# Row halves in turn in the first mixer's score and transpose groups, and the inverse's transfers issued by GpSimd

## The chip, the cores and the metric

The kernel runs on one core of a Trainium2 chip. The metric is the time of one execution on the device in microseconds (us), of which the median over several runs is given. Times inside the program come from one profiled execution of the kernel before; its clock starts with the first instruction of the span.

## The reference, cut to what matters

The program is a two-layer decoder trunk on an input of 1024 tokens by 1024 features, all in float32. Layer 0 is a mixer of eight retention heads and eight RWKV-7 heads, layer 1 is windowed attention, and each is followed by a feed-forward block.

```
for layer in (0, 1):
    h = rms_norm(x)
    x = x + (mixer(h) if layer == 0 else attention(h))
    x = x + swiglu(rms_norm(x))
return rms_norm(x)

mixer(h):
    z = h @ w_in                     # 4*512 columns for retention, 3*512+256 for RWKV
    ret = group_norm(chunk_retention(rotary(q), rotary(k), v)) * silu(g)
    y = rwkv7_scan(r, decay, k, v, -kk, kk * a)
    rwkv = (group_norm(y) + bonus) * gate
    return concat(ret, rwkv) @ w_out

rwkv7_scan, for each token t and head:
    sa = S @ a_t
    S  = S * w_t + outer(sa, b_t) + outer(v_t, k_t)
    y_t = S @ r_t
```

The change touches only how the RWKV-7 heads of `mixer` are computed. The scan is done there in chunks of 64 tokens. In a chunk, the four products of the rows (`AR`: decayed a and r) with the columns (`BK`: decayed b and k) are one matrix product, a "score"; the recursion within the chunk is then the inverse of a unit triangular 64x64 matrix.

## The kernel before, in words

**Stages.** The mixer takes the first 640 us of the 2289 us span, then come the feed-forward block, attention and the second feed-forward block. The sequence is cut in two halves of 512 tokens, and the eight RWKV heads into four pairs of two heads: a head of a pair lies on partitions 0 to 63 (row half e=0), the other on 64 to 127 (e=1). Two pairs of one half of the sequence make a `unit`, so there are units 0 to 3; each inverts the triangles of its two pairs and then runs the recursion.

**Order of TensorE.** All matmuls of the mixer are emitted by generators that the planner `Plan.run` lets advance, but the order in which TensorE executes them is written out in a table, `PE_ORDER`. `pe_order` walks it and ties each matmul behind the one before. A token names a stream, the number of an output tile in that stream, and a count: `i5,6:4` takes the next four matmuls of tiles 5 and 6 of stream i alternately, `i5:2` two of tile 5 alone. Stream F is the mixer's projections (24 matmuls of 128x512 each). Streams f to m are the eight `pair` generators (f, g for unit 0; h, i for unit 1; j, k for unit 2; l, m for unit 3), b to e the four units, n to u the retention pairs. Ahead of the table `pe_order` also ties five single matmuls behind others ("pins"); these lines are the same in both kernels.

**Tiles of a pair.** In a `pair` stream, tiles 5 and 6 are the scores of chunks 0 to 3 for row half e=0 and e=1 (4 matmuls `ps_m<-AR,BK` of 64 rows by 128 each), tiles 7 and 8 the same for chunks 4 to 7, and tiles 9 and 10 the transposes of `BK`, 8 for each row half (`ps_m<-c_ident,BK`, issued by the helper `tr`, L304; the helper `mm`, L293, issues the other matmuls).

**A unit's inverse.** `unit` loads the triangles in 32x32 blocks into `DT`, runs 31 substitution steps on VectorE, writes the blocks `X` to DRAM (`dg`, L976, two transfers), clears the two tiles `GT` on GpSimd (L981), and reads the blocks back into their places with eight transfers (L985). Each has 8x32 pieces of 128 B, 32 KB in all. VectorE transposes `TZ<-GT` (L995, four of them), TensorE multiplies `ps_c<-TZ,GG` (tiles 0 and, from the copies of it, 1 of the unit stream, 32 matmuls for each pair), ScalarE copies, and so on. Each engine takes its instructions strictly in order; the transfers of one issuing queue as well.

**Names.** `qd` is the retention query times its decay (GpSimd, L1199, in place in `r`); TensorE uses it in `ps_m<-r,Sc`. `rr`, `rkk`, `rv` with `z` and `zlast` are the token shift of the RWKV inputs (L756 to L760). `hc<-n` (L1451) are four transfers of attention-layer data that GpSimd issues after the mixer.

Of the kernel before, what the change touches and what calls it, by code (L numbers as in the profile page):

```python
# [10 lines left out]
F32 = mybir.dt.float32  # L11
# [92 lines left out]

PE_ORDER = """
F0:13 F1:2 F0:3 F1:14 F0:3 F1:3 F0:3 F1:3 F0:2 F1:2 F2:2 a0:1 F2:22 F3:24 f0:1 f1:1 F4:24 F5:24 F6:15 f2:1 F6:9
F7:24 g0:1 g1:1 F8:9 f3:16 F8:9 g2:1 F8:6 F9:18 f4:1 F9:6 F10:6 f5,6:8 f7,8:8 F10:17 f9:8 f10:8 f11:16 f12:4
g3:16 f13:4 n0:4 n1:4 g4:1 F10:1 F11:12 f14:16 g5:1 g6:2 g5:2 g6,5:3 g7:1 g8:2 g7:2 F11:12 F12:3 g8,7:3 g9:8
g10:8 F12:13 g11:16 g12:4 n2,3:8 g13:4 F12:8 F13:5 n4:8 n5:8 F13:16 n6:8 g14:16 F13:3 F14:21 n7:1 F14:3 F15:24
F16:6 o0:4 o1:4 F16:18 F17:3 o2,3:8 o4:8 F17:21 o5:1 o6:1 o5:7 b0:32 o6:7 h0:1 h1:1 F18:18 b1:32 o7:1 F18:6  # L110
F19:12 b2:8 h2:1 b3:8 b4:8 F19:12 b5:8 b6:16 b7:8 b8:8 F20:24 F21:13 b9:16 b10:8 h3:16 b11:8 b12:4 F21:8 i0:1
i1:1 b13:4 F21:3 F22:24 F23:6 b14:4 i2:1 F23:6 b20:1 b15:4 b20:15 b21:6 b16:4 b21:4 b22:16 b23:5 F23:9 b23:1
b21:2 b17:4 b23:6 h4:1 F23:3 F24:11 b21:1 b18:4 b21:1 b23:2 h5:4 b21:1 b19:4 b21:1 b23:2 F24:12 h6:4 b24:1 F24:1
F25:24 F26:7 b25:1 b26:1 h7:4 h8:4 b27:1 h9:8 F26:11 h10:8 h11:16 h12:4 i3:16 h13:4 p0:4 F26:6 F27:9 p1:4 i4:1
p2:2 p3:2 p2,3:4 h14:16 i5,6:4 i5:2 i6:2 i7:4 i8:4 F27:15 F28:2 p4:8 i9:8 i10:8 F28:6 i11:16 i12:4 p5:8 p6:8
i13:4 F28:16 F29:19 v0:1 p7:1 i14:16 F29:5 F30:7 q0:4 q1:4 F30:3 F31:2 F30:3 F31:11 q2,3:8 F30:9 F31:6 F30:2
F31:2 q4:8 q5:8 F31:3 F32:6 q6:8 F32:18 F33:22 q7:1 c0:32 F33:2 F34:23 c1:32 F34:1 F35:20 c2:8 c3:8 c4:8 j0:1
F35:4 F36:11 j1:1 c5:8 c6:16 c7:8 c8:8 j2:1 F36:9 c9:16 c10:8 c11:8 c12:2 F36:4 F37:10 c12:2 F37:14 F38:7 j3:5
c13:4 j3:11 k0:1 k1:1 F38:8 c20:5 c14:4 c20:11 c21:6 c22:1 c21:2 c15:4 c22:15 c23:4 c21:2 c23:1 c16:4 c23:5 k2:1
F38:9 F39:8 c17:4 c21:2 c23:2 j4:1 F39:16 F40:2 c21:1 c18:4 c21:1 c23:2 j5:4 c21:1 c19:4 c21:1 c23:2 F40:3 j6:4  # L120
F40:19 F41:12 c24:1 F41:12 F42:24 c25:1 c26:1 j7,8:8 c27:1 j9:8 F43:13 j10:8 j11:16 j12:4 k3:16 j13:4 k4:1
F43:11 F44:11 j14:16 k5,6:8 k7:4 k8:4 F44:9 k9:8 k10:8 k11:16 k12:4 r0:4 r1:4 F44:4 F45:10 k13:4 r2,3:8 r4:8
F45:12 k14:16 r5:8 r6:8 l0:1 l1:1 F45:2 F46:17 r7:1 l2:1 F46:7 F47:24 m0:1 m1:1 F48:24 F49:1 l3:1 F49:17 d0:1
l3:3 d0:31 l3:12 m2:1 d1:32 F49:6 F50:15 d2:8 d3,4:16 d5:8 F50:9 F51:2 d6:16 d7:8 m3:16 d8:8 d9:16 d10:8 d11:8
F51:8 s0,1:8 d12:4 F51:14 F52:2 d13:4 F52:19 s2:1 d14:4 s3,2:7 F52:3 F53:3 d15:4 s4:8 F53:18 s5:2 d16:4 s6:8
d20:3 s5:6 d17:4 d20:13 d21:13 d18:4 d21:1 d22:16 d23:3 d21:1 d19:4 d21:1 d23:13 l4:1 F53:3 F54:14 m4:1 s7:1
l5:3 l6:3 l5:1 l6:1 d24:1 F54:10 F55:17 d25:1 d26:1 F55:7 F56:9 l7:4 l8:4 d27:1 l9:8 l10:8 l11:16 l12:4 m5:3
m6:3 m5:1 m6:1 l13:4 F56:15 m7:2 m8:2 m7,8:4 m9:8 m10:8 t0:4 t1:4 F57:24 m11:16 m12:4 t2:4 e0:2 t3:4 l14:16
m13:4 t4:8 t5:8 t6:4 e0:4 m14:1 t6:4 m14:15 e0:26 F58:24 F59:15 t7:1 e1:32 u0:4 u1:4 F59:9 W0:7 e2:8 e3:8 e4:8
u2:4 W0:17 W1:11 u3:4 e5:8 u4:8 e6:16 e7:8 e8:8 u5:8 u6:8 e9:16 e10:8 e11:8 e12:2 u7:1 e20:5 e12:2 e20:11 e21:4  # L130
e22:6 e13:4 e22:10 e23:4 e21:2 e14:4 e23:2 W1:13 W2:14 e15:4 e21:1 W2:10 W3:13 e21:1 e23:2 e21:1 e16:4 e21:1
e23:2 W3:11 W4:9 e17:4 e21:2 e23:2 W4:15 W5:4 e21:1 e18:4 e21:1 e23:2 W5:20 e19:4 e21:2 W6:24 W7:3 e23:2 e24:1
e25:1 e26:1 e27:1 W7:21
"""


# [121 lines left out]
class Kern:  # L258
# [686 lines left out]
    def unit(self, u, hf, pairs):  # L945

        nc, mp = self.nc, self.mp
        V, S, G = nc.vector, nc.scalar, nc.gpsimd
# [33 lines left out]
        for q in range(8):  # L982
            e, b = (q // 2) % 2, q % 2
            r0 = 64 * e + 32 * b
            nc.sync.dma_start(  # L985
                GTs[q // 4][r0 : r0 + 32, :, 32 * b : 32 * b + 32], dg[q * 8 : q * 8 + 8].rearrange("c s t -> s c t")
            )
        yield tuple((f"a{u}_{p}", 0.0) for p in pairs), 6.0
# [1061 lines left out]
```

## Time and profile before

| | before |
|---|---|
| median of 3 runs | 2292.93 us (2291.54 to 2293.13) |
| profiled execution, device time | 2291.26 us |
| its span, first to last instruction | 2289.4 us |
| granted TensorE clock | 0.999 |
| TensorE busy | 2259.3 us (99% of the span) |
| VectorE, ScalarE, GpSimd busy | 1699.6, 1047.6, 1009.2 us |
| TensorE busy in 0 to 640 us | 624.41 us |
| GpSimd busy in 0 to 640 us | 157.06 us |

A row of a timeline gives the start in us, the length of a run of like instructions, engine, source line, operation, output and inputs, the shape and a count. In square brackets stands how long the engine was idle before it and what released it. A row of a tile view gives the durations of one instruction as minimum/median/maximum in ns, and the first and last start. Line numbers are those of the kernel before; the changed kernel's are one lower from there on, since its table has one line less.

### The profile page before, as it was taken

Reading aid. Unit: us, or ns where it says so; the run is one execution under the profiler, and the core shown is the slowest. Engines: PE = TensorE matmul, PEld = TensorE weight load, DVE = VectorE, ACT = ScalarE, POOL = GpSimd, SP = SyncE. Lnnn points to the kernel's source line nnn. Section 1 sums busy time; section 2 is a strip of 40 time slices with the busy share of each in tenths; the row PEclk is TensorE's granted clock in tenths of the full one; section 3 lists DMA queues with packets and bytes.
Section 4 is the critical chain, followed back from the end, with each engine's and each line's share of the span. In section 5 each row is a group of like instructions: output and inputs, shape, how many; then the busy total and the mean of one; then the engine's idle time right before and its main releaser. Section 6 shows DMA issues by size and latency. Waiting matters only on the chain.

```text
span 2289.4 us, 35743 instructions
## 1 busy us (share of the span) xinstructions
PE 2259.3 (99%) x13056; PEld 1808.5 (79%) x13056; DVE 1699.6 (74%) x2635; ACT 1047.6 (46%) x1947; POOL 1009.2 (44%) x796
## 2 busy tenths in 40 slices
PE   8999999999999999999999999999999999999998
PEld 6777777778878888888788887787788888888886
DVE  7877965876567268887895958857657788888866
ACT  5454544434445333334343466657744333333335
POOL 3123221212340167777776501113203677777675
PEclk9999999999999999999999999999999999999999
DMA  7566554444356455565756332133246466657663
GB/s 279 187 214 210 193 163 128 145 119 132 134 185 221 170 177 205 203 212 211 280 212 239 110 120 79 44 99 118 93 140 230 169 217 213 210 196 284 230 216 116
DMA packets 170336, 406.43 MB, mean 178 GB/s; under 512 B 43184, under 2 KB 45872, under 8 KB 170160
## 3 DMA queue, kind: packets, MB, share of 16 engines
q1 hardware_dynamic: 166752, 397.59, 50.7%
q10 hardware_dynamic: 2832, 4.45, 0.5%
q8 instruction: 104, 1.70, 0.3%
q0 software_dynamic: 576, 2.10, 0.2%
q14 instruction: 72, 0.59, 0.1%
HBM read 275.48 MB, written 123.21 MB: 174 GB/s over the span
## 4 chain that ended last, share of the span: by engine, by line
PE 79%; DVE 10%; ACT 4%; issue 3%; DMA 2%; SPq 1%; POOL 1%; DVEq 0%; ACTq 0%; POOLq 0%
PE ps_f L293 10%; PE ps_m L1302 7%; PE ps_m L1304 7%; PE ps_m L1305 7%; PE ps_m L293 6%; PE ps_f L1302 5%; PE ps_f L1304 5%; PE ps_f L1305 5%; PE ps_f L452 2%; PE ps_f L449 2%; PE ps_f L451 2%; PE ps_r L1302 2%; PE ps_c L1305 2%; PE ps_r L1304 2%; PE ps_c L1304 2%
## 5 line engine op out<-in xcount | busy, mean ns | idle before, releaser
L293 PE MATMUL ps_f<-n,w 128*128 128x512 f32 x1440 | 359.2, 403 | 8.3 <-ACT w L434 5.7
L293 PEld LDWEIGHTS ps_f<-n,w 128*128 128x128 f32 x1440 | 267.4, 189 | 83.0 <-issue 12.6
L435 POOL TENSOR_TENSOR w<-wr,w 128x512 fp32r<-128x512 f32 x63 | 87.0, 1388 | 301.4 <-ACT w L434 293.7
L434 ACT CAST w<-wr 128x512 fp32r<-128x512 f32 x231 | 141.2, 617 | 162.2 <-PE ps_f L452 54.2
L435 DVE TENSOR_TENSOR w<-wr,w 128x512 fp32r<-128x512 f32 x168 | 118.8, 710 | 61.4 <-ACT w L434 60.8
L1302 PE MATMUL ps_f<-n,w 128*128 128x512 f32 x415 | 164.3, 396 | 0.0
L1304 PE MATMUL ps_f<-n,w 128*128 128x512 f32 x415 | 162.7, 392 | 0.0
L1305 PE MATMUL ps_f<-n,w 128*128 128x512 f32 x415 | 162.5, 392 | 0.0
L435 POOL TENSOR_TENSOR w<-wq,w 128x512 fp32r<-128x512 f32 x91 | 130.8, 1448 | 30.9 <-ACT w L434 30.9
L1302 PE MATMUL ps_m<-n,w 128*128 128x512 f32 x333 | 130.4, 392 | 0.0
L1304 PE MATMUL ps_m<-n,w 128*128 128x512 f32 x333 | 129.7, 389 | 0.0
L1305 PE MATMUL ps_m<-n,w 128*128 128x512 f32 x333 | 129.5, 389 | 0.0
L1312 DVE TENSOR_TENSOR nq<-ps_m,u 128x512 f32<-128x512 f32 x88 | 58.9, 684 | 93.8 <-PE ps_m L1305 93.8
L1732 POOL TENSOR_SCALAR s<-s,st 128x256 f32<-128x256 f32 (+1 forms) x32 | 30.7, 961 | 191.1 <-ACT w L434 60.9
L466 POOL TENSOR_TENSOR n<-nq,n 128x512 fp32r<-128x512 f32 x60 | 100.0, 1679 | 7.6 <-ACT n L464 7.6
L1497 POOL TENSOR_TENSOR w<-wd,w 128x512 fp32r<-128x512 f32 (+1 forms) x62 | 87.7, 1423 | 33.5 <-ACT w L1496 31.5
L1302 PEld LDWEIGHTS ps_f<-n,w 128*128 128x128 f32 x415 | 77.9, 188 | 20.4 <-issue 3.8
L1302 PE MATMUL ps_m<-cb,w 128*128 128x512 f32 x236 | 91.9, 389 | 0.4 <-DVE nq L1312 0.4
L1304 PEld LDWEIGHTS ps_f<-n,w 128*128 128x128 f32 x415 | 77.9, 188 | 17.7 <-issue 2.0
L1305 PE MATMUL ps_m<-cb,w 128*128 128x512 f32 x236 | 91.8, 389 | 0.0
L1304 PE MATMUL ps_m<-cb,w 128*128 128x512 f32 x236 | 91.8, 389 | 0.0
L1305 PEld LDWEIGHTS ps_f<-n,w 128*128 128x128 f32 x415 | 77.9, 188 | 16.8 <-issue 0.7
(521 smaller groups left out, 6498.6 us busy)
## 6 DMA issues: line engine op xcount, KB each, us to landing
hc<-n SPq DMA_DIRECT2D x84, 512.0 KB, 3.2
wsp<-w SPq DMA_DIRECT2D x54, 512.0 KB, 3.3
w<-wsp SPq DMA_DIRECT2D x54, 512.0 KB, 3.4
n<-hc SPq DMA_DIRECT2D x54, 512.0 KB, 6.2
wq<-in_w_gate SPq DMA_DIRECT2D x44, 512.0 KB, 4.6
u<-u SPq DMA_DIRECT2D x88, 256.0 KB, 3.3
ha<-hc SPq DMA_DIRECT2D x34, 512.0 KB, 5.3
hid<-n SPq DMA_DIRECT2D x66, 256.0 KB, 2.1
```

The source lines that it names most:

```text
L293: i = self.nc.tensor.matmul(out, lhsT, rhs, **kw)
L434: nc.scalar.copy(hi[:, :n], raw[:, c])
L435: self.lo.tensor_tensor(out=lo[:, :n], in0=raw[:, c], in1=hi.bitcast(F32)[:, :n], op=ALU.subtract)
L449: x = nc.tensor.matmul(ps, hi, rh, start=k == 0, stop=False)
L451: y = nc.tensor.matmul(ps, hi, rl, start=False, stop=False)
L452: z = nc.tensor.matmul(ps, lo, rh, start=False, stop=k == n - 1)
L466: e.tensor_tensor(out=lo, in0=src, in1=hi.bitcast(F32), op=ALU.subtract)
L1302: i = mm(ps, hi, xh, start=first and k == 0, stop=False, skip_group_check=True)
L1304: mm(ps, hi, xl, start=False, stop=False, skip_group_check=True)
L1305: mm(ps, lo, xh, start=False, stop=last and k == len(w) - 1, skip_group_check=True)
L1312: self.last_add = V.tensor_tensor(out=o, in0=x, in1=y, op=ALU.add)
L1497: nc.gpsimd.tensor_tensor(out=lo, in0=v, in1=hi.bitcast(F32), op=ALU.subtract)
```

## The change

Two things change. In `PE_ORDER`, the score groups (tiles 5 and 6, 7 and 8) and the transposes (9 and 10) of the pair streams take the two row halves in turn, at most of the places where they ran one half after the other or in a mixed order. Untouched are f5 to f8, tiles 5, 6, 9 and 10 of h, all of j, and k5,6. In `unit`, the eight transfers `GT<-dg` are issued by GpSimd (`G` is `nc.gpsimd`) in place of SyncE. The table is re-wrapped, so the diff is shown by its tokens:

```
 pair  before                              after
 f     f9:8 f10:8                          f9,10:16
 g     g5:1 g6:2 g5:2 g6,5:3               g5,6:8
       g7:1 g8:2 g7:2 ... g8,7:3           g7,8:5 ... g7:1 g8:2
       g9:8 g10:8                          g9,10:16
 h     h7:4 h8:4                           h7,8:8
 i     i5,6:4 i5:2 i6:2 i7:4 i8:4          i5,6:8 i7,8:8
       i9:8 i10:8                          i9,10:16
 k     k7:4 k8:4 ... k9:8 k10:8            k7,8:8 ... k9,10:16
 l     l5:3 l6:3 l5:1 l6:1                 l5,6:8
       l7:4 l8:4 ... l9:8 l10:8            l7,8:8 ... l9,10:16
 m     m5:3 m6:3 m5:1 m6:1                 m5,6:8
       m7:2 m8:2 m7,8:4 m9:8 m10:8         m7,8:8 m9,10:16
```

```
@@ unit @@
         for q in range(8):
             e, b = (q // 2) % 2, q % 2
             r0 = 64 * e + 32 * b
-            nc.sync.dma_start(
+            G.dma_start(
                 GTs[q // 4][r0 : r0 + 32, :, 32 * b : 32 * b + 32], dg[q * 8 : q * 8 + 8].rearrange("c s t -> s c t")
             )
```

How the instructions stand on TensorE at pair l's second score group and its transposes, before; `ps_m_5490` and `5491` are tiles 7 and 8, `5518` and `5528` tiles 9 and 10:

```order
1577 L293 MATMUL ps_f_5706<-n_456_2935,w_5551 128x512
1578 L293 MATMUL ps_m_5490<-AR_4573,BK_4577 128x128 x4
1579 L293 MATMUL ps_m_5491<-AR_4573,BK_4577 128x128 x4
1580 L293 MATMUL ps_m_5508<-gl_3160,gup_163 128x512
1581 L304 MATMUL ps_m_5518<-c_ident_154,BK_4577 128x64 x8
1582 L304 MATMUL ps_m_5528<-c_ident_154,BK_4577 128x64 x8
```

The same place on TensorE in the changed kernel:

```order
1660 L292 MATMUL ps_f_5706<-n_456_2935,w_5551 128x512
1661 L292 MATMUL ps_m_5490<-AR_4573,BK_4577 128x128
1662 L292 MATMUL ps_m_5491<-AR_4573,BK_4577 128x128
1663 L292 MATMUL ps_m_5490<-AR_4573,BK_4577 128x128
1664 L292 MATMUL ps_m_5491<-AR_4573,BK_4577 128x128
1665 L292 MATMUL ps_m_5490<-AR_4573,BK_4577 128x128
1666 L292 MATMUL ps_m_5491<-AR_4573,BK_4577 128x128
1667 L292 MATMUL ps_m_5490<-AR_4573,BK_4577 128x128
1668 L292 MATMUL ps_m_5491<-AR_4573,BK_4577 128x128
1669 L292 MATMUL ps_m_5508<-gl_3160,gup_163 128x512
1670 L303 MATMUL ps_m_5518<-c_ident_154,BK_4577 128x64
1671 L303 MATMUL ps_m_5528<-c_ident_154,BK_4577 128x64
```

The same eight score matmuls and the same sixteen transposes stand between the same neighbours; only the tile, and with it the row half, now changes with each instruction.

On GpSimd, at unit 0's inverse, before (`X_2530` is the next unit's block tile, which is cleared here, `r_221_1310` the retention query that is multiplied by its decay):

```order
50 L1239 TENSOR_TENSOR r_211_1216<-r_211_1216,r_177_963 128x512
51 L1129 TENSOR_TENSOR r_220_1308<-r_220_1308,c_cos_242 128x512
52 L960 MEMSET X_2530 128x512
53 L962 MEMSET X_2530 64x16 x2
54 L758 COPY zlast_99<-z_1447 128x1
55 L759 TENSOR_TENSOR rr_1446<-z_1447 128x512
56 L1199 TENSOR_TENSOR r_221_1310<-r_221_1310,c_qdec_1393 128x512
```

The same place on GpSimd in the changed kernel (`dg_213` is what the inverse wrote to DRAM):

```order
50 L1238 TENSOR_TENSOR r_211_1216<-r_211_1216,r_177_963 128x512
51 L1128 TENSOR_TENSOR r_220_1308<-r_220_1308,c_cos_242 128x512
52 L984 DMA GT_1422<-dg_213 32x8x32 x4
53 L984 DMA GT_1423<-dg_213 32x8x32 x4
54 L959 MEMSET X_2530 128x512
55 L757 COPY zlast_99<-z_1447 128x1
56 L758 TENSOR_TENSOR rr_1446<-z_1447 128x512
57 L1198 TENSOR_TENSOR r_221_1310<-r_221_1310,c_qdec_1393 128x512
```

Unit 0's eight transfers now stand ahead of the clearing of `X`, of `rr` and of the query's product. In the other units they stand likewise among GpSimd's instructions: in unit 1 ahead of the clearing of `X` and of `rr`, in unit 2 behind `rkk` and ahead of the copy into `z`, the clearing of `X`, `PC` and `AR`, in unit 3 four and four around the product L1239. On SyncE the eight rows `GT<-dg` of each unit are gone; what stood behind them moves up.

More of the change, by code (lines that the diff above doesn't have):

```diff
@@ L106 @@
 F0:13 F1:2 F0:3 F1:14 F0:3 F1:3 F0:3 F1:3 F0:2 F1:2 F2:2 a0:1 F2:22 F3:24 f0:1 f1:1 F4:24 F5:24 F6:15 f2:1 F6:9
[L107 to L130, printed above, removed]
@@ L131 @@
-e22:6 e13:4 e22:10 e23:4 e21:2 e14:4 e23:2 W1:13 W2:14 e15:4 e21:1 W2:10 W3:13 e21:1 e23:2 e21:1 e16:4 e21:1
-e23:2 W3:11 W4:9 e17:4 e21:2 e23:2 W4:15 W5:4 e21:1 e18:4 e21:1 e23:2 W5:20 e19:4 e21:2 W6:24 W7:3 e23:2 e24:1
-e25:1 e26:1 e27:1 W7:21
+F7:24 g0:1 g1:1 F8:9 f3:16 F8:9 g2:1 F8:6 F9:18 f4:1 F9:6 F10:6 f5,6:8 f7,8:8 F10:17 f9,10:16 f11:16 f12:4 g3:16
+f13:4 n0:4 n1:4 g4:1 F10:1 F11:12 f14:16 g5,6:8 g7,8:5 F11:12 F12:3 g7:1 g8:2 g9,10:16 F12:13 g11:16 g12:4
+n2,3:8 g13:4 F12:8 F13:5 n4:8 n5:8 F13:16 n6:8 g14:16 F13:3 F14:21 n7:1 F14:3 F15:24 F16:6 o0:4 o1:4 F16:18
@@ new lines @@
+F17:3 o2,3:8 o4:8 F17:21 o5:1 o6:1 o5:7 b0:32 o6:7 h0:1 h1:1 F18:18 b1:32 o7:1 F18:6 F19:12 b2:8 h2:1 b3:8 b4:8
+F19:12 b5:8 b6:16 b7:8 b8:8 F20:24 F21:13 b9:16 b10:8 h3:16 b11:8 b12:4 F21:8 i0:1 i1:1 b13:4 F21:3 F22:24 F23:6
+b14:4 i2:1 F23:6 b20:1 b15:4 b20:15 b21:6 b16:4 b21:4 b22:16 b23:5 F23:9 b23:1 b21:2 b17:4 b23:6 h4:1 F23:3
+F24:11 b21:1 b18:4 b21:1 b23:2 h5:4 b21:1 b19:4 b21:1 b23:2 F24:12 h6:4 b24:1 F24:1 F25:24 F26:7 b25:1 b26:1
+h7,8:8 b27:1 h9:8 F26:11 h10:8 h11:16 h12:4 i3:16 h13:4 p0:4 F26:6 F27:9 p1:4 i4:1 p2:2 p3:2 p2,3:4 h14:16
@@ new lines @@
+i5,6:8 i7,8:8 F27:15 F28:2 p4:8 i9,10:16 F28:6 i11:16 i12:4 p5:8 p6:8 i13:4 F28:16 F29:19 v0:1 p7:1 i14:16 F29:5
+F30:7 q0:4 q1:4 F30:3 F31:2 F30:3 F31:11 q2,3:8 F30:9 F31:6 F30:2 F31:2 q4:8 q5:8 F31:3 F32:6 q6:8 F32:18 F33:22
+q7:1 c0:32 F33:2 F34:23 c1:32 F34:1 F35:20 c2:8 c3:8 c4:8 j0:1 F35:4 F36:11 j1:1 c5:8 c6:16 c7:8 c8:8 j2:1 F36:9
+c9:16 c10:8 c11:8 c12:2 F36:4 F37:10 c12:2 F37:14 F38:7 j3:5 c13:4 j3:11 k0:1 k1:1 F38:8 c20:5 c14:4 c20:11
+c21:6 c22:1 c21:2 c15:4 c22:15 c23:4 c21:2 c23:1 c16:4 c23:5 k2:1 F38:9 F39:8 c17:4 c21:2 c23:2 j4:1 F39:16
@@ new lines @@
+F40:2 c21:1 c18:4 c21:1 c23:2 j5:4 c21:1 c19:4 c21:1 c23:2 F40:3 j6:4 F40:19 F41:12 c24:1 F41:12 F42:24 c25:1
+c26:1 j7,8:8 c27:1 j9:8 F43:13 j10:8 j11:16 j12:4 k3:16 j13:4 k4:1 F43:11 F44:11 j14:16 k5,6:8 k7,8:8 F44:9
+k9,10:16 k11:16 k12:4 r0:4 r1:4 F44:4 F45:10 k13:4 r2,3:8 r4:8 F45:12 k14:16 r5:8 r6:8 l0:1 l1:1 F45:2 F46:17
+r7:1 l2:1 F46:7 F47:24 m0:1 m1:1 F48:24 F49:1 l3:1 F49:17 d0:1 l3:3 d0:31 l3:12 m2:1 d1:32 F49:6 F50:15 d2:8
+d3,4:16 d5:8 F50:9 F51:2 d6:16 d7:8 m3:16 d8:8 d9:16 d10:8 d11:8 F51:8 s0,1:8 d12:4 F51:14 F52:2 d13:4 F52:19
@@ new lines @@
+s2:1 d14:4 s3,2:7 F52:3 F53:3 d15:4 s4:8 F53:18 s5:2 d16:4 s6:8 d20:3 s5:6 d17:4 d20:13 d21:13 d18:4 d21:1
+d22:16 d23:3 d21:1 d19:4 d21:1 d23:13 l4:1 F53:3 F54:14 m4:1 s7:1 l5,6:8 d24:1 F54:10 F55:17 d25:1 d26:1 F55:7
+F56:9 l7,8:8 d27:1 l9,10:16 l11:16 l12:4 m5,6:8 l13:4 F56:15 m7,8:8 m9,10:16 t0:4 t1:4 F57:24 m11:16 m12:4 t2:4
+e0:2 t3:4 l14:16 m13:4 t4:8 t5:8 t6:4 e0:4 m14:1 t6:4 m14:15 e0:26 F58:24 F59:15 t7:1 e1:32 u0:4 u1:4 F59:9 W0:7
+e2:8 e3:8 e4:8 u2:4 W0:17 W1:11 u3:4 e5:8 u4:8 e6:16 e7:8 e8:8 u5:8 u6:8 e9:16 e10:8 e11:8 e12:2 u7:1 e20:5
@@ L134 @@
+e12:2 e20:11 e21:4 e22:6 e13:4 e22:10 e23:4 e21:2 e14:4 e23:2 W1:13 W2:14 e15:4 e21:1 W2:10 W3:13 e21:1 e23:2
+e21:1 e16:4 e21:1 e23:2 W3:11 W4:9 e17:4 e21:2 e23:2 W4:15 W5:4 e21:1 e18:4 e21:1 e23:2 W5:20 e19:4 e21:2 W6:24
+W7:3 e23:2 e24:1 e25:1 e26:1 e27:1 W7:21
 """
@@ L984, in unit @@
             r0 = 64 * e + 32 * b
-            nc.sync.dma_start(
+            G.dma_start(
                 GTs[q // 4][r0 : r0 + 32, :, 32 * b : 32 * b + 32], dg[q * 8 : q * 8 + 8].rearrange("c s t -> s c t")
```

## The prediction

> **What bounds the kernel now.** I first read the page's busy line and then the windows that part the span at the end of the first mixer (each engine: busy us and instructions).
>
> ```profile
> PE 2259.3 (99%) x13056; PEld 1808.5 (79%) x13056; DVE 1699.6 (74%) x2635; ACT 1047.6 (46%) x1947; POOL 1009.2 (44%) x796
> 0.00:640.00 640.00, 624.41 (x5590) 487.43 (x5590) 458.32 (x951) 293.47 (x475) 157.06 (x190) 1.00 0.53 171
> 640.00:2290.00 1650.00, 1634.87 (x7468) 1321.04 (x7466) 1241.23 (x1685) 754.16 (x1472) 852.11 (x606) 1.00 0.52 180
> ```
>
> TensorE is the bound nearly everywhere. The mixer leaves it 15.6 us idle, GpSimd (POOL) works only 157 of 640 us there. Next I read what TensorE waits for, in the mixer and behind it.
>
> ```profile
> PE ps_f L293 <- ACT w L434: 5.7, 1, 5.7
> PE ps_m L293 <- DVE r L1193: 2.0, 4, 1.3
> PE ps_f L293 <- DVE n L581: 1.7, 2, 1.0
> PE ps_c L293 <- DVE GT L1070: 1.4, 1, 1.4
> PE ps_c L293 <- DVE TZ L995: 0.2, 1, 0.2
> PE ps_m L1742 <- POOL s L1732: 0.9, 3, 0.5
> ```
>
> The largest wait is the start (5.7 us). The transfers that the change moves hold TensorE up for 0.2 us in all, through `TZ`. Behind the mixer the longest entry is 0.9 us, so the later layers have no idle time to swallow a shift: what TensorE gains or loses by the end of the mixer stays to the end. The clock is full throughout (1.00). So the sum has two kinds of terms: matmul groups that get shorter, and waits that GpSimd, now with 32 transfers to issue, makes for TensorE.
>
> **Row halves in turn.** The windows below count only the score matmuls (`AR` an input), with TensorE's busy time and their number. In order they are f5–8, h7,8, i5–8, k5–8, l5,6, l7,8, m5,6 and m7,8.
>
> ```profile
> 73.70:75.80 2.10, 2.04 (x32) 1.00 0.63 208
> 225.30:227.00 1.70, 1.65 (x16) 1.00 0.94 258
> 242.70:245.45 2.75, 2.71 (x32) 1.00 1.03 274
> 401.50:404.10 2.60, 2.57 (x32) 1.00 0.81 244
> 509.70:511.20 1.50, 1.43 (x16) 1.00 0.75 161
> 523.70:525.45 1.75, 1.68 (x16) 1.00 0.59 190
> 529.50:531.00 1.50, 1.46 (x16) 1.00 0.27 102
> 534.95:536.00 1.05, 1.02 (x16) 1.00 0.10 35
> ```
>
> The counts are records, two for a matmul. Where halves alternate already, 16 records take 1.02 us and 32 take 2.04; one half after the other, 16 take 1.65 to 1.68. So alternation takes 0.63 to 0.66 us off a group that ran half by half: h7,8 0.63; i 2.71 − 2.04 = 0.67; k 0.53; l5,6 0.41 and l7,8 0.66; m5,6 0.44; m7,8, largely in turn before, nothing. g's groups were mixed by ones and twos; I give them 0.1.
>
> For the transposes no alternated group exists. The windows are of 8 of one half (h9) and of both halves in sequence (i9,10).
>
> ```profile
> 228.00:228.80 0.80, 0.71 (x8) 1.00 1.04 425
> 250.10:251.20 1.10, 1.02 (x16) 1.00 0.00 0
> ```
>
> If the halves overlap fully, sixteen take what eight take, 0.71; if not at all, 1.02. I take 0.31 us off each of f, g, i, k, l and m, since the score groups do overlap; zero is the other end, 1.9 us in all. The raw sum is 0.31 (f) + 0.41 (g) + 0.63 (h) + 0.98 (i) + 0.84 (k) + 1.38 (l) + 0.75 (m) = 5.3 us.
>
> **What a transfer costs GpSimd.** Before, SyncE issues them; the rows are `GT<-dg` (256 pieces of 128 B), SyncE's transfers of 128 pieces, and the only transfers GpSimd issues, `hc<-n`, 128 pieces of 4 KB, with their landing times.
>
> ```profile
> L985 SPq DMA_DIRECT2D GT<-dg x32: 303/448/1338, 137.9 to 521.2; - x32
> DMA to landing us min/median/max: 1.7/2.3/4.7
> L412 SPq DMA_DIRECT2D w<-wsp x54: 319/326/609, 287.2 to 543.5; - x54
> L1451 POOL DMA_DIRECT2D hc<-n x4: 573/598/739, 1086.2 to 2060.7; - x4
> DMA to landing us min/median/max: 2.9/3.0/3.1
> ```
>
> GpSimd is held 0.598 us by a transfer of 128 pieces. With t for one of ours: if the price goes by transfer, t = 0.60; if by piece, 2 × 0.598 = 1.19. SyncE's ratio of the two kinds is 448/326 = 1.37, so I take t = 0.598 × 1.37 = 0.82, an estimate nearer the low row since the same shapes give that ratio on the one engine where both are seen. Eight hold GpSimd 6.6 us.
>
> The Trainium skill ("DMA: Bandwidth & Descriptors", section "Anatomy of one DMA — SWDGE (gpsimd) path") says that descriptor generation is small and that many descriptors can be emitted before their cost shows. By that, t would be the low end, 0.60; no run here shows a transfer of small pieces issued by GpSimd.
>
> **Unit 0.** The timeline rows of GpSimd behind the inverse's write to DRAM, then two of TensorE:
>
> ```profile
> 137.23 0.53 POOL L960 MEMSET X<- 128x512 f32 x1 [4.62 <-DMA dg<-X]
> 137.81 0.29 POOL L962 MEMSET X<- 64x16 f32 x2
> ...
> 138.69 1.04 POOL L759 TENSOR_TENSOR rr<-z 128x512 f32<-128x512 f32 x1
> 139.69 1.29 POOL L1199 TENSOR_TENSOR r<-r,c_qdec 128x512 f32<-128x512 f32 x1
> ...
> 142.39 0.43 PE L293 MATMUL ps_m<-r,Sc 64*64 64x128 f32 x2
> 144.94 0.69 PE L293 MATMUL ps_c<-TZ,GG 32*32 32x32 f32 x30 [0.22 <-DVE TZ L995]
> ```
>
> `dg` lands at 137.2. Before, the decayed query is done at 139.69 + 1.29 = 140.98 and TensorE takes it at 142.39 without a wait. In the changed order the eight transfers stand ahead of `X`, `rr` and the query; one small clearing (0.29 + gap) now falls behind it, so it is done at about 140.5 + 8t, and TensorE waits 8t − 1.9 us: 2.9 at 0.60, 4.7 at 0.82, 7.6 at 1.19. `TZ` (last issue 137.2 + 7t, landing 2.3 to 3.0, 0.44 to transpose) is ready about when the query is, and hides behind it. VectorE, with `TZ` now ahead of `rr` L760, has its weights' conversions late by less than that. What f and g gain (0.72) lies before this wait, which runs from the inverse's chain on VectorE, and is counted at nothing.
>
> **Unit 1.** GpSimd's first row behind the write, the last transpose of `TZ`, and TensorE's use of it:
>
> ```profile
> 296.02 0.53 POOL L960 MEMSET X<- 128x512 f32 x1 [1.32 <-DMA dg<-X]
> 300.90 0.44 DVE L995 STREAM_TRANSPOSE TZ<-GT 32x256 f32<-32x256 f32 x1 [0.42 <-DMA GT<-dg]
> 301.33 1.20 PE L293 MATMUL ps_c<-TZ,GG 32*32 32x32 f32 x64
> ```
>
> TensorE needs the second half of `TZ` in mid-group, near 301.9. Now the last transfer is issued at 296.0 + 7t, lands some 2.5 later (between the two rows), and 0.44 goes to the transpose: 298.9 + 7t, so a wait of 7t − 3.0 (1.2, 2.7, 5.3). h's 0.63 comes ahead of the triangles and is kept; i's 0.98 comes behind them, brings TensorE to the wait sooner, and is lost in it.
>
> **Units 2 and 3.** SyncE's issue in unit 2, TensorE's use, and the last transpose and the first use in unit 3:
>
> ```profile
> 439.39 3.77 SPq L985 DMA_DIRECT2D GT<-dg  x8
> 449.35 0.82 PE L293 MATMUL ps_c<-TZ,GG 32*32 32x32 f32 x40
> 525.36 0.44 DVE L995 STREAM_TRANSPOSE TZ<-GT 32x256 f32<-32x256 f32 x1
> 546.17 0.25 PE L293 MATMUL ps_c<-TZ,GG 32*32 32x32 f32 x4
> ```
>
> In unit 2 the last landing moves to about 439.4 + 7t + 2.5 = 447.6, the transpose to some 448.6 behind the copy into `z` that now waits for GpSimd: in time at 0.82, about 1.3 us late at 1.19. k's 0.84 may be met by that or by short waits for VectorE; I keep half, 0.4. Unit 3 has 20 us to spare, and l's and m's 2.1 us stay. Queues: SyncE loses 32 issues of 0.45 us, so that the loads behind them (`w<-wsp` and unit 3's rotary copies `r<-r`) go earlier; I give 0.4 for the short waits on them, with zero as the other end. GpSimd's rows behind its transfers are those named: `X`, `rr`, the query in unit 0, `z`, `PC`, `AR` in unit 2.
>
> **Sum.** At t = 0.82: +4.7 + 2.7 − 0.6 − 0.4 − 2.1 − 0.4 = +3.9 us. On the profiled execution of 2291.26 us that is 2295.2; the median, 1.67 us above it, becomes 2296.8. At 0.60 the sum is 2.9 + 1.2 − 3.5 = +0.6; at 1.19 7.6 + 5.3 + 1.3 − 3.1 = +11.1 (k's gain lost too).
>
> **The rivals.** *Price by transfer alone*: t = 0.60, +0.6 us, 2293.5. For it: 0.598 is the only price of GpSimd's that the trace shows. Against: SyncE's own price rises with the pieces. It is the skill's rule that stands above.
>
> *Price by piece (slower)*: t = 1.19 at GpSimd in units 0 and 1 makes TensorE wait 7.6 and 5.3 us; +11.1, 2304.0. It decides for slower from t = 0.87 on, where the sum passes 4.6 us. For it: software that writes pieces one at a time would do this. Against: nothing that the trace holds; it has one shape only.
>
> *Price by bytes (faster)*: `hc<-n` moves 512 KB for 0.598, ours 32 KB. If most of that goes with bytes, t is near 0.25 (a guess of order, between nothing and 0.60): unit 0 waits 0.1, unit 1 not, i's gain is kept, and the sum is 0.1 − 0.6 − 1.0 − 0.8 − 2.1 − 0.4 = −4.8, 2288.1. Against: it needs the query within 1.9 us of what it has now.
>
> *The halves in turn don't save what they show*: without the 3.1 us that the sum counts for them, +7.0, 2299.9. Against: eight windows say otherwise.
>
> **Numbers.** Forecast (t between 0.70 and 0.95, +2.1 to +5.8, 2295.0 to 2298.7) 0.38; by transfer 0.18; by piece 0.30; by bytes 0.10; no saving 0.04. A change within 0.2%, 4.6 us, is about what a measurement of this kernel can't tell from none. The forecast case lies two thirds within it: same 0.25 + 0.18 = 0.43, slower 0.13 + 0.30 + 0.04 = 0.47, faster 0.10. The range leaves out the faster rival and the far end of the by-piece one: 2290.5 to 2304.
>
> **What would show it.** GpSimd's rows `GT<-dg`: their mean is t. TensorE's waits: a new one before `ps_m<-r,Sc` near 142 on GpSimd's query, and one on `TZ` near 302. Score windows of 16 records at 1.02 us, transposes of 16 at 0.71. I am wrong if the query's wait is under 2 us or above 7, if unit 2 makes TensorE wait by over 1 us, or if the groups keep their old length.

## The result, and the profile after

| | before | after |
|---|---|---|
| median | 2293.03 us (2291.54 to 2295.17, 4 runs) | 2314.93 us (2312.10 to 2315.82, 4 runs) |
| ratio, 95% interval | | 1.0096 (1.0084 to 1.0108) |
| profiled execution, span | 2291.26, 2289.4 us | 2312.10, 2310.3 us |
| granted TensorE clock | 0.999 | 0.993 |

The changed kernel is about 22 us slower, far outside the forecast range that ended at 2304. The waits of TensorE in the mixer of the changed kernel (engine, tile and line, what it waited for: us in all, times, longest) show three entries, of 8.2, 6.4 and 3.2 us, that were 0.2 us or less before:

```profile
PE ps_m L292 <- POOL r L1198: 8.2, 1, 8.2
PE ps_c L292 <- DVE TZ L994: 6.4, 5, 1.8
PE ps_m L303 <- DVE GG L886: 3.2, 3, 2.4
```

A ledger by place comes from one group that stands once in each unit, TensorE's second inverse product. Its start in units 0 to 3 before, and then after:

```profile
151.93 1.20 PE L293 MATMUL ps_c<-GT,TZ 32*32 32x32 f32 x64
308.36 1.20 PE L293 MATMUL ps_c<-GT,TZ 32*32 32x32 f32 x64
452.37 1.20 PE L293 MATMUL ps_c<-GT,TZ 32*32 32x32 f32 x64
563.58 1.20 PE L293 MATMUL ps_c<-GT,TZ 32*32 32x32 f32 x64
```
```profile
163.49 1.20 PE L292 MATMUL ps_c<-GT,TZ 32*32 32x32 f32 x64
324.25 1.20 PE L292 MATMUL ps_c<-GT,TZ 32*32 32x32 f32 x64
473.41 1.20 PE L292 MATMUL ps_c<-GT,TZ 32*32 32x32 f32 x64
586.22 1.20 PE L292 MATMUL ps_c<-GT,TZ 32*32 32x32 f32 x64
```

TensorE is 11.6 us late behind unit 0, 15.9 behind unit 1, 21.0 behind unit 2 and 22.6 behind unit 3. At the end of the program the span is 20.9 us longer: as forecast, the later layers take little back (1.7 us). Such a ledger compares two single executions, and they differ by themselves: two of the kernels below, the order alone and unit 3 alone, are the same up to unit 3, and yet stand 1.5 us apart behind unit 0 and 3.9 behind unit 2. So differences of 2 to 4 us between two traces prove nothing unless a wait shows them.

**Unit 0.** The timeline of GpSimd in the changed kernel, from the landing of `dg`, two rows of VectorE, and the transfers in the tile view (durations in ns):

```profile
138.23 1.98 POOL L984 DMA_DIRECT2D GT<-dg  x3 [5.47 <-DMA dg<-X]
143.52 1.16 POOL L984 DMA_DIRECT2D GT<-dg  x2 [3.31 <-issue]
146.10 1.79 POOL L984 DMA_DIRECT2D GT<-dg  x3 [1.42 <-issue]
147.88 0.54 POOL L959 MEMSET X<- 128x512 f32 x1
...
149.49 1.26 POOL L1198 TENSOR_TENSOR r<-r,c_qdec 128x512 f32<-128x512 f32 x1
```
```profile
143.23 0.43 DVE L994 STREAM_TRANSPOSE TZ<-GT 32x256 f32<-32x256 f32 x1 [2.38 <-DMA GT<-dg]
145.81 0.43 DVE L994 STREAM_TRANSPOSE TZ<-GT 32x256 f32<-32x256 f32 x1 [1.39 <-DMA GT<-dg]
```
```profile
L984 POOL DMA_DIRECT2D GT<-dg x32: 582/584/814, 138.2 to 546.7; - x32
```

One transfer holds GpSimd 0.584 us, near the 0.60 of the rival "by transfer" and under the forecast 0.82. But after three of them it stands for 3.31 us and again for 1.42. Its own row names no releaser ("issue"), but the rows of VectorE do: the first `TZ` needs the first transfer and starts with its landing at 143.23, and GpSimd issues the fourth at 143.52; the second `TZ` needs the third transfer, starts at 145.81, and the sixth is issued at 146.10. So three transfers are under way, and the next one goes out 0.3 us after one of them has landed; the other three units show the same. It is not VectorE's work that holds GpSimd up, for VectorE is idle for 2.38 of the 3.31 us. The eight take 9.65 us (138.23 to 147.88), 1.2 us each. TensorE, in the rows below, waits 8.19 us for the query, and then runs every group at about twice its length (the 14 took 1.09 us before):

```profile
150.80 0.69 PE L292 MATMUL ps_m<-r,Sc 64*64 64x128 f32 x2 [8.19 <-POOL r L1198]
151.41 1.97 PE L292 MATMUL ps_m<-r,r 128*64 128x128 f32 x14
153.31 1.92 PE L292 MATMUL ps_c<-TZ,GG 32*32 32x32 f32 x64
```
```profile
152.00:159.00 7.00, 7.00 (x94) 0.50 0.04 11
```

The window's row shows why (its stretch, length, TensorE's busy time and records, then the granted clock, 0.50). From windows of 1 us each, half clock begins at 145.70, in the middle of the wait, and ends at 159.36.

**When half clock comes.** Read in the same way, this trace has three more stretches of half clock in the mixer: 285.66 to 289.06, 316.38 to 319.78 and 469.98 to 473.38. They last 3.4 us, the first one four times that, and from one beginning to the next it is 41, 9 and 45 times 3.413 us. The experiments' traces agree: eleven of the twelve kernels with a changed order or changed transfers have such stretches in the mixer, 38 in all, of 3.4, 6.8, 10.2, 13.7 or 17.1 us, and in each trace they begin and end on one grid of 3.41 us, whose place differs from trace to trace. So what counts is TensorE's idle time within one step of that grid. From 24 us to the end of the mixer, all 24 steps at full clock with 1.70 us of it or more were followed by half clock, 14 of 38 with 1.20 to 1.70 us, and none of some 2200 with less (idle times are rough, since the ends of matmuls are modelled).

**Units 1 to 3.** In units 1 and 2 it is `TZ` that comes late, with half clock behind the wait. Ahead of unit 1's inverse, at 285.69, another wait has grown, from 0.98 to 2.37 us for the input `n` of the projections, with half clock behind it too. In unit 3 TensorE uses `TZ` 20 us later, as forecast, and yet waits: in the changed kernel's timelines of VectorE and TensorE,

```profile
546.44 0.43 DVE L994 STREAM_TRANSPOSE TZ<-GT 32x256 f32<-32x256 f32 x1 [2.54 <-DMA GT<-dg]
549.27 1.28 DVE L886 TENSOR_TENSOR GG<-ps_m,c_gmask 128x512 f32<-128x512 f32 x2
```
```profile
545.17 1.16 PE L292 MATMUL ps_m<-AR,BK 64*128 64x128 f32 x16
547.32 0.27 PE L303 MATMUL ps_m<-c_ident,BK 64*128 64x64 f32 x1
550.01 0.71 PE L303 MATMUL ps_m<-c_ident,BK 64*128 64x64 f32 x15 [2.42 <-DVE GG L886]
558.41 0.66 PE L303 MATMUL ps_m<-c_ident,BK 64*128 64x64 f32 x16
```

VectorE, in order, stands 2.54 us before a transpose `TZ` that nobody needs yet, and only behind it empties the PSUM banks (the parts of the memory into which TensorE writes) of l's scores (`GG`). The transposes of `BK` in turn need a second bank with their second instruction; that bank is not free. Part of this wait belongs to the new order itself: 1.36 us of it is there with the order alone, whose transfers are not late (below).

The groups did get shorter: l7,8 takes 1.09 us to the next start (1.64 before), and sixteen transposes in turn run in 0.66 us where a bank is there (558.41; 0.94 before).

### The profile page after: what moved, and what is told of

The parts are those of the page before. It is cut to its first block, busy times and chain, and to the rows that moved or that the text cites. A ratio compares the mean times of both kernels' runs of the same rounds, so it can differ in the third digit from the quotient of the medians.

```text
span 2310.3 us, 35776 instructions
## 1 busy us (share of the span) xinstructions
PE 2263.6 (98%) x13056; PEld 1810.0 (78%) x13056; DVE 1696.8 (73%) x2635; ACT 1047.6 (45%) x1947; POOL 1025.2 (44%) x828
## 4 chain that ended last, share of the span: by engine, by line
PE 77%; DVE 10%; ACT 4%; issue 3%; DMA 3%; POOL 2%; SPq 1%; DVEq 0%; ACTq 0%; POOLq 0%
PE ps_f L292 9%; PE ps_m L1301 8%; PE ps_m L1304 7%; PE ps_m L1303 7%; PE ps_f L1301 5%; PE ps_f L1303 5%; PE ps_f L1304 5%; PE ps_m L292 5%; PE ps_f L451 2%; PE ps_f L450 2%; PE ps_f L448 2%; PE ps_r L1301 2%; PE ps_c L1304 2%; PE ps_r L1304 2%; PE ps_c L1301 2%
## 5 line engine op out<-in xcount | busy, mean ns | idle before, releaser
L292 PEld LDWEIGHTS ps_f<-n,w 128*128 128x128 f32 x1440 | 269.3, 191 | 85.2 <-issue 12.6
L1301 PEld LDWEIGHTS ps_f<-n,w 128*128 128x128 f32 x415 | 77.9, 188 | 20.3 <-issue 3.8
L1303 PEld LDWEIGHTS ps_f<-n,w 128*128 128x128 f32 x415 | 77.9, 188 | 17.8 <-issue 2.0
L1496 POOL TENSOR_TENSOR w<-ws,w 128x512 fp32r<-128x512 f32 (+1 forms) x48 | 71.3, 1491 | 45.0 <-ACT w L1495 41.2
```

The source lines that it names most:

```text
L292: i = self.nc.tensor.matmul(out, lhsT, rhs, **kw)
L1301: i = mm(ps, hi, xh, start=first and k == 0, stop=False, skip_group_check=True)
L1303: mm(ps, hi, xl, start=False, stop=False, skip_group_check=True)
L1496: nc.gpsimd.tensor_tensor(out=lo, in0=v, in1=hi.bitcast(F32), op=ALU.subtract)
```

## The experiments

All times below are from the same chips as their own runs of the kernel before (medians 2290.78, 2291.36 and 2291.45 us in the three groups).

**The two parts, and the units, apart.** Four kernels: the table alone; the transfers alone; the changed kernel with only unit 0's transfers on GpSimd; and with all but unit 0's.

```
order_only:   PE_ORDER changed;  nc.sync.dma_start(GTs...)
gpsimd_only:  PE_ORDER as before;  G.dma_start(GTs...)
gp_unit0:     (G if u == 0 else nc.sync).dma_start(GTs...)
gp_not0:      (nc.sync if u == 0 else G).dma_start(GTs...)
```

> The changed kernel's order of TensorE, with the transfers GT<-dg issued by SyncE as before. Theory (the loss is GpSimd's transfers; the row halves in turn save 0.3 us in a transpose group and 0.5 in a score group where no bank is waited for): 1 to 3 us faster than before (2290 to 2292), no wait at ps_m<-r,Sc near 142, and the groups of h, k and of the transposes as short as in the changed kernel. Rival (both halves in turn need two PSUM banks at once, and VectorE empties them no faster, so that the groups' gain comes back as waits for GG): the same time as before within 1 us. Second rival (the wait of 2.4 us before l's transposes comes from the order and not from late transfers): it is there too, and the time is 1 us above before.

> The order of TensorE as before, the 32 transfers GT<-dg issued by GpSimd. Theory (nearly the whole loss is theirs): 20 to 25 us slower than before (2313 to 2318), with the wait of 8 us before ps_m<-r,Sc near 142 and TensorE's clock at 0.5 behind it. Rival (the order and the transfers lose together, through banks that come free late): 10 to 17 us slower.

> The changed kernel, but only unit 0's eight transfers are issued by GpSimd, the others by SyncE. Theory (unit 0 costs 11.3 us: 8.2 of wait and 3.2 of slow clock, and nothing of it is given back later): 8 to 11 us slower than before. Rival (a shift by the first unit is taken up by later waits): 3 us slower or less.

> The changed kernel, but unit 0's transfers are issued by SyncE; those of units 1 to 3 by GpSimd. Theory (unit 1 costs 5.3 us, unit 2 5.6, both on TZ, the order gives some 1 to 3 back): 8 to 11 us slower than before, and with the kernel that has unit 0's alone the two losses add up to the changed kernel's 22 within 3 us, counting the order's share once. Rival (the losses are not additive): the sum is off by more than 5.

| kernel | ratio to before, 95% interval | us |
|---|---|---|
| order alone | 1.0008 (0.9999 to 1.0017) | +1.8 |
| transfers alone | 1.0122 (1.0108 to 1.0136) | +28 |
| unit 0 on GpSimd | 1.0065 (1.0050 to 1.0081) | +15 |
| units 1 to 3 on GpSimd | 1.0056 (1.0043 to 1.0070) | +13 |

The transfers are nearly the whole loss: without them the kernel is by its interval at most 3.9 us slower. All three kernels with transfers on GpSimd came out slower than expected (28 for 20 to 25, 15 and 13 for 8 to 11 each). The order alone gains nothing: the first theory's 1 to 3 us is refuted. The rival, the same time within 1 us, lies in the interval, but its reason (banks) is only a part. The second rival is half right: a wait for `GG` before l's transposes is there too, of 1.36 us.

```profile
528.26 0.71 PE L303 MATMUL ps_m<-c_ident,BK 64*128 64x64 f32 x15 [1.36 <-DVE GG L886]
```

TensorE's rows of the order alone earlier in the mixer, the window's granted clock there, and the same two rows before:

```profile
284.58 0.43 PE L292 MATMUL ps_m<-r,r 128*64 128x128 f32 x2 [1.26 <-DVE r L1192]
285.34 1.61 PE L292 MATMUL ps_m<-r,r 128*64 128x128 f32 x14 [0.33 <-DVE r L1192]
286.00:288.00 2.00, 2.00 (x11) 0.50 0.81 280
```
```profile
286.08 0.43 PE L293 MATMUL ps_m<-r,r 128*64 128x128 f32 x2 [1.26 <-DVE r L1193]
286.84 1.09 PE L293 MATMUL ps_m<-r,r 128*64 128x128 f32 x14 [0.33 <-DVE r L1193]
```

TensorE comes here 1.50 us earlier than before and waits exactly as long, but now half clock follows: the 14 take 1.61 us in place of 1.09, and at 290.2 the lead is gone. That the lead came from the order is not shown, since the kernel with unit 3 alone, the same up to there, stands at 286.09. In unit 2 an old wait for a weight load grows from 0.18 to 1.68 us (1.91 and 1.93 in the two other kernels with this order and unit 2's transfers on SyncE). SyncE now issues `cat<-r` between the two writes of `dg`, so that `GT<-dg` goes at 441.31 (439.39 before), and the loads `w<-wsp` behind it go later:

```profile
437.37 0.65 SPq L1239 DMA_DIRECT2D cat<-r  x1
441.31 3.78 SPq L984 DMA_DIRECT2D GT<-dg  x8
448.61 1.65 PE L292 MATMUL ps_f<-n,w 128*128 128x512 f32 x6 [1.68 <-DMA w<-wsp]
```

The two parts by units add up to 27.7 − 1.8 (the order once) = 26 against 22, outside the 3 us expected and inside the rival's 5; the intervals of the terms, 2 to 3.5 us each, allow both. The traces show two places where the excess can sit. With unit 0's transfers on GpSimd alone TensorE loses 4.2 us between the markers of units 1 and 2, at that wait of 1.91 us and half clock behind it. With unit 0's on SyncE it is still 3.8 us late behind unit 0, at two waits for `TZ` of 1.83 and 0.39 us and half clock. The transfers alone, with the order as before, are 6 us slower than the changed kernel: in the traces 6.8 us of this lie between the markers of units 2 and 3, where the transfers alone ran at half clock for 17 us and the changed kernel not at all.

**What stops GpSimd after three.** The same transfers with half the pieces each:

```
-GTs[q // 4][r0 : r0 + 32, :, ...], dg[q * 8 : q * 8 + 8]
+GTs[q // 4][r0 : r0 + 32, 0:4, ...], dg[q * 8 : q * 8 + 4]
```

> The changed kernel, each of the 32 transfers carrying only chunks 0 to 3 (128 pieces in place of 256; the other half of the blocks is left out, so the output is not the reference's). In the changed kernel GpSimd issued three at 0.58 us each and then stood for 3.3 us before the next, so that eight took 9.65 us. Theory (there is room for a number of pieces in flight, some 770 of them): now six go in a row, the eight take 5 to 6 us, the query's wait in unit 0 falls from 8.2 to 3 to 4.5 us, and the time is 8 to 14 us below the changed kernel's. Rival (room for a number of transfers, three): three and a gap again, the eight take 8 us or more and the time stays within 3 us of the changed kernel's. Second rival (the price is by piece): 0.3 us each.

Unit 0 on GpSimd and the wait on TensorE, and the transfers' durations:

```profile
136.65 4.03 POOL L984 DMA_DIRECT2D GT<-dg  x7 [4.36 <-DMA dg<-X]
141.71 0.56 POOL L984 DMA_DIRECT2D GT<-dg  x1 [1.03 <-issue]
145.18 0.43 PE L292 MATMUL ps_m<-r,Sc 64*64 64x128 f32 x2 [3.00 <-POOL r L1198]
L984 POOL DMA_DIRECT2D GT<-dg x32: 551/551/764, 136.6 to 530.0; - x32
```

Seven go in a row, where the theory had six; the eighth waits 1.03 us, until the first has landed (VectorE's first `TZ` starts at 141.42). The burst takes 5.6 us and the wait falls from 8.19 to 3.00. The ratio is 1.0028 (1.0017 to 1.0039), +6.4 us: some 16 us below the changed kernel, more than the 8 to 14 expected. So the limit is one of pieces in flight: 3 × 256 = 768 and 7 × 128 = 896 were under way at once, 1024 in no burst of the two traces. In unit 1 all eight go in a row, but there the first has landed at 305.73 and the eighth is issued at 306.8. A limit of three transfers is refuted. The price by piece is too: 0.551 and 0.584 us for 128 and 256. The halved transfers have half the bytes as well; against a limit of bytes, under 128 KB by these numbers, speaks that each `hc<-n` carries 512 KB in 128 pieces and holds GpSimd no longer (0.598 us).

**The clock.** The changed kernel with matmuls repeated in front of the query's wait, 24 and then 37 of them (the table's token `o5:1` becomes `o5:25` and `o5:38`):

```
 self.mm(p1[a, c, :], vt[:, c, e, :], sc[e][:, c, :], start=True, stop=True)
+if (hf, p, c, e) == (0, 1, 0, 0):
+    for _ in range(24):     # 37
+        x = nc.tensor.matmul(p1[a, c, :], vt[:, c, e, :], sc[e][:, c, :], start=True, stop=True)
+        self.order(p1, x)
```

> The changed kernel with 24 more matmuls on TensorE in unit 0, a repetition of the one that stands ahead of the wait for the query (same result, its output is not touched); they fill that wait. Theory (TensorE's clock falls to half while it stands idle and comes back only some 9 us after it works again): the clock stays at 1.00 from 142 to 160, the rows behind the wait have their length of before (1.09 us for the 14, 1.2 for the 64 of TZ,GG) and the time is 3 to 3.6 us below the changed kernel's. Rival (the rows are long for another reason, such as late weights or operands): their length stays and so does the time, within 1 us.

> As the kernel with 24 repeated matmuls, but 37 of them: at 0.225 us each, as 24 took 5.4 us, they fill the 8.2 us of the query's wait. With 24 a wait of 2.6 us was left, and TensorE ran 6 us at half clock behind it. Theory (half clock follows any idle time of some 2 us, so that no idle time means no half clock): a wait of 0.5 us or less, clock 1.00 from 142 to 165, the 14 rows behind it in 1.09 us and TZ,GG's 64 in 1.2, and unit 0's shift against before falls from 11.2 to 8.3 us or less. Rival (the clock falls for another reason, such as the kind of the rows): half clock stays, and the shift stays within 1 us of 10.

TensorE's rows with 24, then with 37:

```profile
149.63 0.43 PE L292 MATMUL ps_m<-r,Sc 64*64 64x128 f32 x2 [2.60 <-POOL r L1198]
151.21 1.92 PE L292 MATMUL ps_c<-TZ,GG 32*32 32x32 f32 x64
```
```profile
150.91 0.43 PE L292 MATMUL ps_m<-r,Sc 64*64 64x128 f32 x2 [0.90 <-POOL r L1198]
151.27 1.09 PE L292 MATMUL ps_m<-r,r 128*64 128x128 f32 x14
152.28 1.20 PE L292 MATMUL ps_c<-TZ,GG 32*32 32x32 f32 x64
159.80 1.20 PE L292 MATMUL ps_c<-GT,TZ 32*32 32x32 f32 x64
```

With 24 a wait of 2.60 us was left, and half clock came all the same, which the theory had not expected. With 37 the wait is 0.90 us, a little over the 0.5 expected, the clock stays at 1.00 and the groups have their old length. TensorE is then 7.9 us late (159.80 against 151.93), 3.7 less than the changed kernel's 11.6. The wait ends at nearly the same time in both (150.91 and 150.80), and from there to the marker this run takes 8.89 us, the changed kernel 12.69: the clock's share is 3.8 us. In the medians (2317.15 and 2313.88 us; ratios 1.0118, 1.0102 to 1.0134, and 1.0099, 1.0085 to 1.0112) such a share does not stand out from the spread of units 1 to 3; the evidence is the trace.

**The query ahead of the burst.** Unit 0's transfers pinned behind the query's product on GpSimd:

```
+*((("gt", 0, i), ("qd", 0, 1)) for i in range(8))      # pins in pe_order
```

> The changed kernel with unit 0's eight transfers pinned behind the product of the query on GpSimd, the others as they are. Theory (unit 0's loss is GpSimd's order: the query queued behind the burst): the wait at ps_m<-r,Sc goes; the burst starts at 141 in place of 138.2 and ends near 150, so TZ is what is late, and TensorE waits for it 5 to 7 us near 144, in pieces. With a lower clock behind it as before the gain is only 0 to 3 us on the changed kernel. Rival (the query is the whole of unit 0's loss, TZ is hidden): 8 to 11 us faster than the changed kernel.

The ratio is 1.0105 (1.0089 to 1.0121), 2315.33 us: no gain, so the rival is refuted. The query's wait is gone and `TZ` takes its place, in four pieces of 8.4 us together (5 to 7 had been expected), the last of which shows in TensorE's row:

```profile
153.32 1.06 PE L292 MATMUL ps_c<-TZ,GG 32*32 32x32 f32 x30 [4.42 <-DVE TZ L994]
```

So the burst itself is late, whichever of its two results TensorE needs first.

**Another engine's queue.** `nc.scalar.dma_start` in place of `G.dma_start`:

> The changed kernel with the transfers issued by ScalarE's queue in place of GpSimd's. Theory (the loss belongs to GpSimd's way of issuing, not to leaving SyncE): each issue takes ScalarE about 0.45 us with no gap of 3 us, no wait for the query, and the time is within 3 us of the kernel before. Rival (any engine with work of its own delays it and TensorE by the eight issues of 3.6 us, and they wait there for dg's landing with what is queued behind): 5 to 12 us slower than before.

The ratio is 1.0034 (1.0021 to 1.0047), +8 us. The first theory expected 3 at most; the time is in the rival's range. Issue and wait, from the timelines of ScalarE and TensorE:

```profile
137.64 5.70 ACTq L984 DMA_DIRECT2D GT<-dg  x8
143.43 1.66 ACT L433 CAST w<-wr 128x512 fp32r<-128x512 f32 x3 [7.85 <-DMA GT<-dg]
145.49 1.99 PE L292 MATMUL ps_c<-TZ,GG 32*32 32x32 f32 x62 [1.55 <-DVE TZ L994]
```

No gap of 3 us here, but ScalarE's own work stands 7.85 us, 5.70 of them for the issues, and behind a wait of 1.55 us the 62 take 1.99 us (64 took 1.2), at a granted clock of 0.50. Both engines that were tried, each with work of its own, lose something by these transfers; ScalarE loses about a third of what GpSimd does.

**Unit 3 alone.** The changed order, `(G if u == 3 else nc.sync).dma_start`:

> The changed order of TensorE, only unit 3's eight transfers issued by GpSimd. TensorE uses their result 20 us later. Theory (the transposes TZ stand on VectorE ahead of l's score masks GG, and through the late transfers VectorE empties l's PSUM banks late): a wait of 1.5 to 3 us for GG before l's transposes (l9,10) and 1 to 3 us slower than the kernel with the changed order alone. Rival (20 us of slack hide it): no such wait over 0.5 us, and the same time as that kernel.

```profile
530.41 0.43 DVE L994 STREAM_TRANSPOSE TZ<-GT 32x256 f32<-32x256 f32 x1 [2.45 <-DMA GT<-dg]
533.99 1.11 PE L303 MATMUL ps_m<-c_ident,BK 64*128 64x64 f32 x15 [2.45 <-DVE GG L886]
535.03 1.97 PE L292 MATMUL ps_m<-c_ident,AR 64*64 64x64 f32 x32
```

The wait is there, with half clock behind it (1.97 us where 1.15 stood before). But 1.36 us of wait stand there with the order alone, so that the late transfers add some 1.1 us, and the half clock, which the order alone does not have at this place. The ratio is 1.0011 (1.0001 to 1.0020), against 1.0008 for the order alone: the medians, 2294.47 and 2292.17, differ the expected way but their intervals overlap. The wait is shown, its effect on the whole time is not.

**Only the late groups in turn.** The kernel before with four tokens changed:

```
-l5:3 l6:3 l5:1 l6:1   l7:4 l8:4   m5:3 m6:3 m5:1 m6:1   m9:8 m10:8
+l5,6:8                l7,8:8      m5,6:8                m9,10:16
```

> The kernel before, with the row halves in turn only at l5,6, l7,8, m5,6 and m9,10, whose gains nothing later in the mixer waits for; l9,10 stay one half after the other, and SyncE issues the transfers. Theory (gains that no bank and no other engine's work absorb stay to the end): the four groups shorten by 0.33, 0.55, 0.33 and 0.30 us and TensorE is 1.0 to 1.5 us ahead of before from 540 us on; in the median that is 0 to 2 us, at the edge of what can be measured. Rival (VectorE's emptying of the banks sets the pace there): the groups shorten, waits for GG or r grow by as much, and TensorE is less than 0.5 us ahead.

The ratio is 1.0002 (0.9993 to 1.0011). The time agrees with the rival and does not exclude the theory. In the trace TensorE gains 0.3 us on the kernel before from l's first scores to the last marker, where the theory had 1.0 to 1.5; its rows:

```profile
528.84 0.71 PE L303 MATMUL ps_m<-c_ident,BK 64*128 64x64 f32 x8 [0.72 <-DVE GG L886]
537.25 0.67 PE L303 MATMUL ps_m<-c_ident,BK 64*128 64x64 f32 x16
538.19 1.25 PE L303 MATMUL ps_m<-c_ident,r 128*128 128x128 f32 x8 [0.28 <-DVE GG L886]
```

The groups are shorter, waits for `GG` of 0.72 and 0.28 us, which were not there before, follow them. No kernel here beats the one before.

## Why the prediction was wrong, point by point

- **The price of a transfer.** Forecast 0.82 us, measured 0.584: the rival "by transfer" was right about the issue itself. So was the rule of the Trainium skill weighed there ("DMA: Bandwidth & Descriptors", section "Anatomy of one DMA — SWDGE (gpsimd) path"). The step that failed is "eight hold GpSimd 6.6 us". I multiplied a price by a count, as if a queue had no end. The burst took 9.65 us: the fourth transfer, which would have made 1024 pieces in flight, waited until the first had landed, and so on. The four `hc<-n` of 128 pieces showed nothing of it.
- **Unit 0.** The chain was right (query behind burst, `TZ` hidden behind the query), the size was not: a wait of 8.19 us in place of 4.7, and then 3.8 us of half clock, which the sum had no term for. A wait above 7 us was one of the prediction's own signs of being wrong. The Trainium skill ("TensorE: Matmul & The Clock Gate", section "HAM oscillation — how this bites in real kernels") warns of idle gaps above some 3.4 us; my own forecast of 4.7 us should have set it off. Here less was enough: half clock followed waits of 2.60, 1.55 and, in the order alone, of 1.26 and 0.33 together, which had not brought it before; it did not follow one of 1.68. With 1.70 us or more of idle time in one step it came each time; with 1.2 to 1.7 us it came in some executions and not in others, and what decides there stays open.
- **Unit 1.** Forecast 2.7 us of wait and i's gain lost in it; TensorE lost 4.3 us from unit 0's marker to unit 1's, at waits for `n` and `TZ` of up to 2.4 us and two stretches of 3.4 us at half clock.
- **Unit 2.** Forecast in time, and it cost 5.1 us. At 7t + 2.5 the last landing was near; with the burst stretched, `TZ` was late twice (1.73 and 1.60 us), with half clock behind.
- **Unit 3.** "20 us to spare" looked at the consumer only. The failed step is that I did not ask what stands behind `TZ` on VectorE: l's bank, which the transposes in turn need earlier than the old order did.
- **Row halves.** The groups shortened nearly as forecast (0.30 us of 0.31 for transposes, 0.55 of 0.66 for l7,8). That h's, l's and m's gains are kept is what failed: the order alone is +1.8 us (−0.2 to +3.9), not −3. In its profiled execution half clock behind an old wait took 1.5 us; in unit 2 the wait for a weight load grew by 1.5 us; in the late groups waits for `GG` took what was won.
- **The rivals.** "By piece" had 11.1 us and the right sign, by luck, from the wrong cause; the pieces count, but as room and not as time.

## What to carry to other kernels

Before transfers are moved to another queue, ask how many pieces are in flight at once, not only what an issue costs; and ask what stands in order behind each instruction that waits for them, on their consumer's engine too. A wait of 2 us on TensorE can cost more than itself: where that much idle time fell into one step of 3.41 us, half clock followed every time. And a group made shorter on the bound engine pays only if its banks are emptied as fast and nothing behind it is paced by another engine: look at the waits that are there already.

## What the runs showed of the hardware

GpSimd's issue costs 0.55 to 0.58 us whether a transfer has 128 or 256 pieces. At most 768 pieces (of 256 to a transfer) and 896 (of 128) were in flight at once; the next issue then stood until a transfer had landed, and went 0.3 to 0.4 us later. TensorE's half clock came in whole steps of 3.41 us on a fixed grid, after 1.70 us or more of idle time in a step each time, after less than 1.20 never; one to five steps followed, and what sets their number stays open. Thirty-seven matmuls repeated in the wait kept the clock at 1.00. Sixteen 64-row transposes of both halves in turn take 0.66 us, about the time of eight of one half (0.71).
